# Value weights multiplied into the output weights, and attention over the latent rows: one edit to a hybrid encoder-layer kernel

## The chip, the cores and the metric

The program runs on one core of one Trainium2 chip. What is compared is the device time of one execution in microseconds (us), the median of several runs. TensorE (PE in the profile) does the matmuls, VectorE (DVE), ScalarE (ACT) and GpSimd (POOL) the elementwise work; SyncE (SP) issues nearly all DMA transfers, ACT's queue a few. Each engine executes its own instructions strictly in order and waits for the others on semaphores.

## The reference, cut to what matters

One encoder layer over 2048 tokens of width 1024, in float32. Two head groups work on one input projection `z`: a bidirectional mLSTM and a latent attention (MLA) with 4 heads. Their outputs are joined, multiplied by `w_out` and added to `x`; a feed-forward block follows. The part that the change touches:

```python
kv = (rms_norm(c_kv, g_ckv) @ w_ukv).reshape(B, S, A_HEADS, A_NOPE + A_DV)   # 128 -> 4 x (128 + 128)
k_nope, v = kv[..., :A_NOPE], kv[..., A_NOPE:]
...
s = jnp.einsum('bhqd,bhkd->bhqk', q_blk, kh) * scale
p = jax.nn.softmax(s, axis=-1)
out = jnp.einsum('bhqk,bhkv->bhqv', p, vh)
...
x = x + jnp.concatenate([y_a, y_b], axis=-1) @ w_out[l]                      # y_b = out, 4 x 128 columns
```

The latent `c_kv` has 128 columns, and it is the same for all heads; a head's value is `c_kv @ Wv_h` with a 128x128 matrix. Since `p @ (c Wv_h) @ Wo_h = (p @ c) @ (Wv_h Wo_h)`, the value projection of the tokens can be replaced by a product of two weight matrices for each head.

## The kernel before, in words

Every float32 matrix product is done as three matmuls on operands split into a high part (rounded to the matmul's format, a cast on ACT) and a low part (the rest, a subtraction on DVE or POOL): `split` (L53, L54; with a gain L56, L57) makes the parts, `mm3` (L69 to L71) issues the matmuls high x high, high x low, low x high. Tiles have 128 partitions and up to 512 columns.

The program has four stages, with places that matter here in the first two.

1. **Input stage** (`phase_a`, to about 458 us of the profile). Two halves of 8 token tiles (128 tokens each). A half first projects each tile onto the "rest" columns (gates, latents, rotary key), then runs three blocks of 8 steps with the weights of the mLSTM's values (`z_v`), queries and keys (`z_qk`) and output gate (`z_o`). A step is 24 matmuls into a bank `pz`. `tick` hangs the MLA work of a tile between the steps: `mla_a1` normalises the latents (`cn`) and transposes them, `mla_a2` multiplies them by `w_ukv` (two banks of 512 columns, tiles `wukh`, `wukl`, result `pm`) and `w_uq`, `mla_b1` and `mla_b2` apply norms and rotary factors and store queries and keys; `mla_b1` also copies the values out (L369) and stores them to `d_va` (L371). The last `z_qk` blocks end with a convolution, `ot`, that is transposed (L464), copied (`kt`, one buffer, L466 and L478) and stored to `d_k` (L471, L472, L479). The order on each engine in this stage is chosen by the framework's scheduler from its own cost estimates, so an edit can move instructions anywhere in the stage, up to the first rows of the next one.
2. **Attention** (`attention`, about 458 to 1110 us). The order is the written one. Step g of 256 computes one 128x512 block of scores, five matmuls into one of three banks `ps` (L1090 to L1094); DVE scales it, takes the maximum and frees the bank (L1095); ACT applies the exponential (L1106). From step 16 on, blocks of probabilities are transposed (`ptp`, L1137) and split, from step 22 on multiplied with the values (`pv`). Keys are loaded and split once a head, and so are values (`load_v`, `split_v`: 4 tiles for each of 4 heads). `work` is a generator that issues one piece of the mLSTM for each step: its first 28 pieces (`mlstm_prelude`) work out the gate tables in short chains on PE, DVE and ACT, with steps in which nothing is issued; the rest (`mlstm_steps`) are the chunks. The prelude's matmuls use the two banks `pm`.
3. **Output projection** (`OutProj`): `concat(y_a, y_b) @ w_out`, with Strassen-like products. It loads the rows of `w_out` below 512 for `y_b` at L1381 and L1497.
4. **Feed-forward** (`FeedForward`), untouched.

SP's queue is in order: a DMA instruction that waits for its data or its buffer holds up all that are behind it.

Of the kernel before, what the change touches and what calls it, by code (L numbers as in the profile page):

```python
# [88 lines left out]
def scratch(c, ctx):  # L89
# [9 lines left out]
    c.d_kr = dr.tile([NH, ROPE, S], F32, name="d_kr")  # L99
    c.d_va = dr.tile([S, 512], F32, name="d_va")  # L100
    c.d_ya = dr.tile([S, 512], F32, name="d_ya")
# [17 lines left out]
def phase_a(c):  # L119
    nc, tc = c.nc, c.tc  # L120
    with ExitStack() as st:
# [136 lines left out]
        def load_wu():  # L258
            for k in range(2):
                for j in range(2):  # L260
                    raw = rp.tile([P, 512], F32, name="raw")
                    cs = slice(j * 384, (j + 1) * 384)
                    nc.sync.dma_start(raw[:, :384], c.w_uq[k * P:(k + 1) * P, cs])
                    split(nc, wuqh[k][:, cs], wuql[k][:, cs], raw[:, :384], gcq[:, k:k + 1])
            for j in range(2):
                raw = rp.tile([P, 512], F32, name="raw")
                cs = slice(j * 512, (j + 1) * 512)
                nc.sync.dma_start(raw, c.w_ukv[:, cs])
                split(nc, wukh[:, cs], wukl[:, cs], raw, gcq[:, 2:3])

# [38 lines left out]
        def mla_a1(t, zr):  # L309
# [18 lines left out]
            with urgent():  # L328
                split(nc, ch, cl, pt[:, 0:3, :])
            mla_env[t] = [zr, ms3, ch, cl]  # L330

        def mla_a2(t):

            zr, ms3, ch, cl = mla_env[t]
            pk, pq = [], []
            for j in range(2):
                o = psM.tile([P, 512], F32, name="pm")
                cs = slice(j * 512, (j + 1) * 512)
# [11 lines left out]
            qs = [pq[h // 2][:, (h % 2) * DH:(h % 2 + 1) * DH] for h in range(NH)]  # L350
            ks = [pk[h // 2][:, (h % 2) * 256:(h % 2) * 256 + NOPE] for h in range(NH)]
            for h in range(NH):
# [7 lines left out]
            rsqrt(c, r8, ms8, 8)  # L360
            mla_env[t] = [zr, pk, qs, ks, r8]

        def mla_b1(t):

            tok = slice(t * P, (t + 1) * P)
            zr, pk, qs, ks, r8 = mla_env[t]
            vn = mp.tile([P, NH, DV], F32, name="vn")
            for j in range(2):
                nc.scalar.copy(vn[:, 2 * j:2 * j + 2, :],  # L369
                               pk[j].rearrange("p (h d) -> p h d", h=2)[:, :, NOPE:])  # L370
            nc.sync.dma_start(c.d_va[tok, :], vn.rearrange("p h d -> p (h d)"))  # L371
            kpe = mp.tile([P, 1, ROPE], F32, name="kpe")
# [141 lines left out]
        rbs = {}  # L514
# [18 lines left out]
        for half in range(2):  # L533
# [35 lines left out]
            for blk in range(3):  # L569
# [35 lines left out]
def mlstm_prelude(c, psM):  # L605
# [4 lines left out]
    with ExitStack() as st:  # L610
# [111 lines left out]
        stores(1)  # L722
        yield


# [13 lines left out]
def mlstm_steps(c, pool, ps, ld):  # L739
# [185 lines left out]
    for n, grp in enumerate(groups):  # L925
        outs = [outer(kws.pop(ch), ld.pop(ch)[0]) for ch in grp]
        yield
        for k, ch in enumerate(grp):
            new = back[ch - 1] = advance(1, NT - 1 - ch, outs[k])
            if ch > 4:  # L930
                nc.sync.dma_start(c.d_C[ch - 1], new)
                ld[ch - 4] = mlstm_v(c, ch - 4), mlstm_k(c, ch - 4)
            if k == 0 and n + 1 < len(groups):
# [69 lines left out]
def attention(c, keep, drain, project):  # L1003

    nc, tc = c.nc, c.tc
    with ExitStack() as st:
# [41 lines left out]

        def load_v(h, j):
            raw = vraw[h, j] = rp.tile([P, 512], F32, name="raw").rearrange("p (k d) -> p k d", k=4)  # L1050
            nc.sync.dma_start(raw, c.d_va[j * 512:(j + 1) * 512, h * DV:(h + 1) * DV].rearrange(
                "(k p) d -> p k d", p=P))

        def split_v(h, j):
            raw = vraw.pop((h, j))
# [3 lines left out]
            V[h, j] = vh, vl  # L1059

# [80 lines left out]
        def pv(b, j, k):  # L1141
            h = b // NB
# [3 lines left out]
            vh, vl = V[h, j]  # L1146
            if b < N - 1:
# [34 lines left out]
        load_v(0, 0)  # L1182
        load_v(0, 1)
        work = mlstm()
        def next_v(bp, j):
            h = bp // NB + 1
            if bp % NB == NB - 1 and h < NH:
                split_v(h, j)
                if j < 2:
                    load_v(h, j + 2)  # L1190

        for g0 in range(0, 16 * N, 2):
# [4 lines left out]
            for g in pair:  # L1197
                bp, n = divmod(g - 22, 16)
                if bp >= 0:
                    pv(bp, *divmod(n, 4))  # L1200
                    if n % 4 == 3:
                        next_v(bp, n // 4)
            if g0 % 16 == 4 and g0 > 32:
                out(g0 // 16 - 2)()
            for g in pair:
# [8 lines left out]
                if h < NH - 1 and i == 7 and u in (4, 5, 6):  # L1214
                    split_k(h + 1, u - 3, nc.vector if u == 6 else nc.gpsimd)
                    if u == 6:
                        load_v(h + 1, 0)
                        load_v(h + 1, 1)
                if g >= 16:
# [13 lines left out]
                if h < NH - 1:  # L1233
# [4 lines left out]
                    if i == 6 and u in (4, 5, 6):  # L1238
                        load_k(h + 1, u - 3)
                if g in (6, 8, 10, 12):  # L1240
                    split_v(0, g // 2 - 3)
                    if g < 10:
                        load_v(0, g // 2 - 1)
            if g0 == 16 * N - 10:
# [96 lines left out]
class OutProj:  # L1341
# [19 lines left out]
    def weights(self):  # L1361
# [132 lines left out]
    def load_b2(self, half):  # L1494
        for k in range(4):
            self.c.nc.sync.dma_start(self.c.e[:, 4 * (1 - half) + k, :],
                                     self.c.w_out[(4 + k) * P:(5 + k) * P, half * 512:(half + 1) * 512])  # L1497

# [848 lines left out]
```

## Time and profile before

| what | us |
|---|---|
| median of 3 runs | 2544.44 (2542.18 to 2544.75) |
| the profiled execution's own time | 2542.08 |
| its span, first to last instruction | 2540.3 |
| PE busy | 2523.7 (99%) |
| DVE busy | 1726.1 (68%) |
| ACT busy | 1293.7 (51%) |
| POOL busy | 380.7 (15%) |

The profile's busy time of an engine is the time covered by its instructions, whether or not they overlap; a matmul's row has its length from first to last column, and the next one may start before it ends. In lists of instructions by time the first column is the start, the second the length, and behind the instruction stands the idle time before it with what ended it; `x2` means that neighbours of one kind were merged into a row. `SPq` and `ACTq` are DMA instructions on those queues. The granted clock of TensorE is 1.00 in all windows.

### The profile page before, as it was taken

Reading aid. Unit: us, or ns where it says so; the run is one execution under the profiler, and the core shown is the slowest. Engines: PE = TensorE matmul, PEld = TensorE weight load, DVE = VectorE, ACT = ScalarE, POOL = GpSimd, SP = SyncE. Lnnn points to the kernel's source line nnn. Section 1 sums busy time; section 2 is a strip of 40 time slices with the busy share of each in tenths; the row PEclk is TensorE's granted clock in tenths of the full one; section 3 lists DMA queues with packets and bytes.
Section 4 is the critical chain, followed back from the end, with each engine's and each line's share of the span. In section 5 each row is a group of like instructions: output and inputs, shape, how many; then the busy total and the mean of one; then the engine's idle time right before and its main releaser. Section 6 shows DMA issues by size and latency. Waiting matters only on the chain. (4 is left out here: it accounts for less than half of the span.)

```text
span 2540.3 us, 35812 instructions
## 1 busy us (share of the span) xinstructions
PE 2523.7 (99%) x12380; PEld 2111.3 (83%) x12380; DVE 1726.1 (68%) x3286; ACT 1293.7 (51%) x2900; POOL 380.7 (15%) x428
## 2 busy tenths in 40 slices
PE   9999999999999999999999999999999999999999
PEld 7888888788888888888888888888888888888887
DVE  5585467766667667678788777977775577665433
ACT  6454444656767677674455555655554323332332
POOL 1211111223323332200000000000000232322000
PEclk9999999999999999999999999999999999999999
DMA  5434234355344343235786555654448544444552
GB/s 177 143 112 152 91 113 137 111 146 134 89 115 114 85 121 102 63 110 193 235 271 227 196 189 185 244 166 149 142 153 300 201 149 142 145 145 145 211 183 95
DMA packets 295931, 392.53 MB, mean 155 GB/s; under 512 B 32262, under 2 KB 176965, under 8 KB 295749
## 3 DMA queue, kind: packets, MB, share of 16 engines
q1 hardware_dynamic: 293284, 385.78, 48.0%
q10 hardware_dynamic: 2464, 4.46, 0.5%
q8 instruction: 97, 1.59, 0.3%
q14 instruction: 86, 0.70, 0.1%
HBM read 258.51 MB, written 131.64 MB: 154 GB/s over the span
## 5 line engine op out<-in xcount | busy, mean ns | idle before, releaser
L69 PE MATMUL pd<-w2h,uh 128*128 128x512 f32 x896 | 348.8, 389 | 0.1
L70 PE MATMUL pd<-w2l,uh 128*128 128x512 f32 x896 | 348.7, 389 | 0.0
L71 PE MATMUL pd<-w2h,ul 128*128 128x512 f32 x896 | 348.7, 389 | 0.0
L54 DVE TENSOR_TENSOR ul<-ur,uh 128x1024 fp32r<-128x1024 f32 x110 | 149.3, 1357 | 251.8 <-ACT uh L53 251.8
L53 ACT CAST uh<-ur 128x1024 fp32r<-128x1024 f32 x110 | 115.7, 1052 | 396.0 <-PE pd L70 382.4
L54 DVE TENSOR_TENSOR ptl<-ptp,pth 128x512 fp32r<-128x512 f32 x248 | 171.1, 691 | 190.0 <-ACT pth L53 188.9
L53 ACT CAST pth<-ptp 128x512 fp32r<-128x512 f32 x248 | 143.4, 578 | 157.7 <-PE ptp L1137 157.1
L2015 DVE TENSOR_TENSOR e<-pu,e 128x512 f32<-128x512 f32 x224 | 151.3, 689 | 88.7 <-PE pu L71 87.7
L69 PEld LDWEIGHTS pd<-w2h,uh 128*128 128x128 f32 x896 | 168.2, 188 | 35.4 <-DVE e L2015 0.5
L71 PEld LDWEIGHTS pd<-w2h,ul 128*128 128x128 f32 x896 | 168.2, 188 | 34.9
L70 PEld LDWEIGHTS pd<-w2l,uh 128*128 128x128 f32 x896 | 168.2, 188 | 34.8
L1106 ACT ACTIVATE p<-p,nm 128x512 f32<-128x512 f32 x256 | 185.8, 726 | 2.6 <-DVE nm L1099 2.6
L1095 DVE TENSOR_SCALAR_CACHE_REDUCE p<-ps 128x512 f32<-128x512 f32 x256 | 167.4, 682 | 15.2 <-PE ps L1094 15.1
L2179 POOL TENSOR_TENSOR r<-wr,r 128x512 f32<-128x512 f32 x48 | 81.5, 1697 | 621.1 <-DMA wr<-in_w 590.0
L69 PE MATMUL pz<-wh,hh 128*128 128x512 f32 (+1 forms) x384 | 149.5, 391 | 1.7 <-ACT vo L495 0.7
L71 PE MATMUL pz<-wh,hl 128*128 128x512 f32 (+1 forms) x384 | 150.0, 391 | 0.0
L70 PE MATMUL pz<-wl,hh 128*128 128x512 f32 (+1 forms) x384 | 149.2, 389 | 0.1
L2018 ACT ACTIVATE e<-e 128x512 f32<-128x512 f32 x128 | 80.9, 632 | 120.5 <-DVE e L2015 114.0
L1137 PE MATMUL ptp<-ident,p 128*128 128x128 f32 x992 | 130.6, 274 | 0.5 <-DVE ptl L54 0.3
L1137 PEld LDWEIGHTS ptp<-ident,p 128*128 128x128 f32 x992 | 113.6, 140 | 14.1 <-issue 1.4
L1090 PE MATMUL ps<-kh,qh 128*128 128x512 f32 x256 | 112.8, 441 | 2.4 <-DVE p L1095 2.4
L1883 ACT CAST r<-w1raw 128x512 fp32r<-128x512 f32 x104 | 64.6, 622 | 92.5 <-PE pu L71 92.5
(526 smaller groups left out, 6463.5 us busy)
## 6 DMA issues: line engine op xcount, KB each, us to landing
d_u<-e SPq DMA_DIRECT2D x224, 256.0 KB
ur<-d_u SPq DMA_DIRECT2D x110, 512.0 KB
wr<-in_w SPq DMA_DIRECT2D x96, 256.0 KB
w1raw<-in_w SPq DMA_DIRECT2D x42, 512.0 KB
raw<-in_w_in SPq DMA_DIRECT2D x48, 256.0 KB
r<-in_w SPq DMA_DIRECT2D x22, 512.0 KB
mb<-d_M SPq DMA_DIRECT2D x32, 256.0 KB
acc<-d_x SPq DMA_DIRECT2D x16, 512.0 KB
```

Source lines behind the costliest of these rows:

```text
L53: r = nc.scalar.copy(hi, src)
L54: (eng or nc.vector).tensor_tensor(lo, src, hi.bitcast(F32), op=ALU.subtract)
L69: nc.tensor.matmul(out, ah, bh, start=first, stop=False, skip_group_check=more)
L70: nc.tensor.matmul(out, ah, bl, start=False, stop=False, skip_group_check=more)
L71: nc.tensor.matmul(out, al, bh, start=False, stop=last, skip_group_check=more)
L1090: nc.tensor.matmul(o, qh[:, qs], kh, start=True, stop=False)
L1095: nc.vector.tensor_scalar(p, o, SCALE, None, op0=ALU.mult, op1=ALU.max, accum_out=maxes[b, a][:, j:j + 1])
L1106: nc.scalar.activation(p, p, AF.Exp, bias=maxes[b, a], accum_out=dens[b][:, a, j:j + 1])
L1137: nc.tensor.transpose(pt[:, k, :], p[:, k * P:(k + 1) * P], c.ident)
L2015: nc.vector.tensor_tensor(out, o, t, op=ALU.add)
L2018: nc.scalar.activation(t, t, AF.Relu)
L2179: nc.gpsimd.tensor_tensor(R, wr, R, op=ALU.subtract)
```

## The change

* `mla_a2` multiplies the latents by the key columns of `w_ukv` alone: `wukh` and `wukl` hold 512 columns (head by head the first 128 of 256), one bank instead of two. The normalised latent `cn[:, 256:384]` is stored to a new array `d_cn` (64 KB a tile) from ACT's queue. `mla_b1` no longer copies values out, and `d_va` is gone.
* `value_rows`, new, works out `Wv_h Wo_h` for the 4 heads: it loads the value columns of `w_ukv` (`wv`), multiplies them by the norm's gain on POOL, transposes them on PE (4 transposes), splits them, and for each of 8 pieces (head, half of the columns) loads 128x512 of `w_out` (`wraw`), splits it (ACT, POOL: `wo0`, `wo1`), issues three matmuls into `pm`, copies the result out on DVE and stores it to `d_wv`. It is a generator beside the prelude: both advance once a step. Its transposes come at step 3 (counted from 0), the first split of a piece at step 4, products 0 to 4 at steps 6, 8, 10, 12, 14 and products 5 to 7 at steps 22, 24, 26. Like the prelude it has 28 pieces.
* Attention uses `d_cn` as the values of all heads: `load_v` and `split_v` run 4 times instead of 16, at steps 2 to 8 and 16 to 22.
* The first mLSTM loads (`d_v`, `d_k`) are issued at step 10 instead of step 0, later ones one piece earlier.
* One more of the three key splits at a head's end runs on DVE instead of POOL.
* The output projection reads its lower rows from `d_wv`.
* In the input stage, `x` tiles have 3 buffers instead of 2; tiles 8 to 10 are loaded at step 3 of the third block of the first half, and tiles 11 to 15 three tiles ahead.

```diff
-        xp = pool("a_x", 2, "right")
+        xp = pool("a_x", 3, "right")
...
         def mla_a2(t):
-            zr, ms3, ch, cl = mla_env[t]
-            pk, pq = [], []
-            for j in range(2):
-                o = psM.tile([P, 512], F32, name="pm")
-                cs = slice(j * 512, (j + 1) * 512)
-                mm3(nc, o, ch[:, 2, :], cl[:, 2, :], wukh[:, cs], wukl[:, cs], True, True)
-                pk.append(o)
+            zr, ms3, ch, cl, cn = mla_env[t]
+            nc.scalar.dma_start(c.d_cn[t * P:(t + 1) * P, :], cn[:, 256:384])
+            pq = []
+            pk = psM.tile([P, 512], F32, name="pm")
+            mm3(nc, pk, ch[:, 2, :], cl[:, 2, :], wukh[:, 0:512], wukl[:, 0:512], True, True)
...
         def mla_b1(t):
-            vn = mp.tile([P, NH, DV], F32, name="vn")
-            for j in range(2):
-                nc.scalar.copy(vn[:, 2 * j:2 * j + 2, :],
-                               pk[j].rearrange("p (h d) -> p h d", h=2)[:, :, NOPE:])
-            nc.sync.dma_start(c.d_va[tok, :], vn.rearrange("p h d -> p (h d)"))
...
+            elif 8 <= t < 13:
+                xts[t + 3] = load_x(t + 3)
...
+                    if half == 0 and blk == 2 and i == 3:
+                        for t in range(8, 11):
+                            xts[t] = load_x(t)
...
+def value_rows(c, pool, psM):
+    outs = [tile([P, 512], F32, name=f"wst{i}") for i in range(2)]
+    pieces = [tile([P, 512], F32, name=f"wraw{i}") for i in range(3)]
+    raw = tile([P, NH, P], F32, name="wv")
+    wvh, wvl = (tile([P, NH, P], F32R, name=f"wv{u}") for u in "hl")
+    homes = [[tile([P, 512], F32R, name=f"wo{i}{u}") for u in "hl"] for i in range(2)]
...
+    def load(n):
+        if n < 2 * NH:
+            r, cs = place(n)
+            nc.sync.dma_start(pieces[n % 3], c.w_out[512:][r, cs])
+
+    def part(n):
+        if n < 2 * NH:
+            split(nc, *homes[n % 2], pieces[n % 3], eng=nc.gpsimd)
+            load(n + 3)
+
+    nc.sync.dma_start(raw, c.w_ukv.rearrange("p (h t d) -> p h t d", h=NH, t=2)[:, :, 1, :])
+    for n in range(3):
+        load(n)
+    for _ in range(2):
+        yield
+    nc.gpsimd.tensor_scalar(raw, raw, c.vec[:, 10:11], None, op0=ALU.mult)
+    yield
+    pt = psM.tile([P, 512], F32, name="pm").rearrange("p (k t) -> p k t", k=4)
+    for h in range(NH):
+        nc.tensor.transpose(pt[:, h, :], raw[:, h, :], c.ident)
+    yield
+    split(nc, wvh, wvl, pt)
+    part(0)
+    yield
+    yield
+    store = None
+    for n in range(2 * NH):
+        o = psM.tile([P, 512], F32, name="pm")
+        mm3(nc, o, wvh[:, n // 2, :], wvl[:, n // 2, :], *homes[n % 2], True, True)
+        if store:
+            nc.sync.dma_start(*store)
+        yield
+        w = outs[n % 2]
+        nc.vector.tensor_copy(w, o)
+        store = c.d_wv[place(n)], w
+        part(n + 1)
+        yield
+        for _ in range(6 if n == 4 else 0):
+            yield
+    nc.sync.dma_start(*store)
...
-            ld = {ch: (mlstm_v(c, ch), mlstm_k(c, ch)) for ch in range(NT - 1, NT - 5, -1)}
-            yield from mlstm_prelude(c, psM)
+            with ExitStack() as s_fold:
+                fold = value_rows(c, pool("w_sb", 1, "left", s_fold.enter_context), psM)
+                for n, _ in enumerate(mlstm_prelude(c, psM)):
+                    next(fold, None)
+                    if n == 10:
+                        ld = {ch: (mlstm_v(c, ch), mlstm_k(c, ch)) for ch in range(NT - 1, NT - 5, -1)}
+                    yield
+                for _ in fold:
+                    yield
...
-                    split_k(h + 1, u - 3, nc.vector if u == 6 else nc.gpsimd)
+                    split_k(h + 1, u - 3, nc.gpsimd if u == 4 else nc.vector)
...
-            nc.sync.dma_start(raw, c.w_out[k * P:(k + 1) * P, :])
+            nc.sync.dma_start(raw, c.d_wv[(k - 4) * P:(k - 3) * P, :])
```

Three places where the order of instructions moves. The first is PE in the middle of the input stage, where one token tile's latents (`cTh`, `cTl`) meet the key and value weights (`wukh`, `wukl`) and the query weights (`wuqh`, `wuql`). Before:

```order
L69 MATMUL pm<-wukh,cTh 128x512
L70 MATMUL pm<-wukl,cTh 128x512
L69 MATMUL pm<-wukh,cTh 128x512
L70 MATMUL pm<-wukl,cTh 128x512
L69 MATMUL pm<-wuqh_152,cTh 128x384
L70 MATMUL pm<-wuql_154,cTh 128x384
```

Now, at the last tile:

```order
L69 MATMUL pm<-wukh,cTh 128x512
L70 MATMUL pm<-wukl,cTh 128x512
L69 MATMUL pm<-wuqh_153,cTh 128x384
L71 MATMUL pm<-wukh,cTl 128x512
L70 MATMUL pm<-wuql_155,cTh 128x384
```

A tile issues three matmuls with `wukh` and `wukl` instead of six (before, the two with `cTl` follow some rows later).

The second is SP's queue where the input stage ends: `ot` and `kt` are the last convolution blocks of the mLSTM's keys, `v` and `knat` the mLSTM's first loads, `wv` and `wraw` the new loads. Before:

```order
L459 DMA d_qkT<-ot 128x514
L479 DMA d_k<-kt 2x128
L471 DMA d_k<-kt 128x128
L472 DMA d_k<-kt 128x3x128
L728 DMA v_4979<-d_v 128x4x128
L479 DMA d_k<-kt 2x128
L735 DMA knat_4983<-d_k 128x256
```

Now:

```order
L453 DMA d_qkT<-ot 128x514
L465 DMA d_k<-kt 128x128
L466 DMA d_k<-kt 128x3x128
L473 DMA d_k<-kt 2x128
L750 DMA wv<-in_w_ukv 128x4x128
L743 DMA wraw_4973<-in_w_out 128x512
```

The load of `wv` stands directly behind the last store of `kt`, where the first load of `d_v` and `d_k` stood around it.

The third is PE at the start of attention: `pz` is the last step of the input stage, `ps` a block of scores, `pt<-ident,ot` the transposes from which `kt` is copied, `pm<-ident,G` the prelude's first matmuls. Before:

```order
L69 MATMUL pz<-wh,hh 128x512
L464 MATMUL pt<-ident,ot 128x128 x4
L476 MATMUL pt<-ident,ot 2x128
L70 MATMUL pz<-wl,hh 128x512
L71 MATMUL pz<-wh,hl 128x512
L69 MATMUL pz<-wh,hh 128x512
L70 MATMUL pz<-wl,hh 128x512
L71 MATMUL pz<-wh,hl 128x512
L1094 MATMUL ps<-rl,qr 128x512
```

Now, from the second block of scores on:

```order
L1151 MATMUL ps<-rl,qr 128x512
L458 MATMUL pt<-ident,ot 128x128 x4
L470 MATMUL pt<-ident,ot 2x128
L627 MATMUL pm<-ident,G 64x128
L628 MATMUL pm<-rev,G 64x128
L627 MATMUL pm<-ident,G 64x128
L628 MATMUL pm<-rev,G 64x128
L1147 MATMUL ps<-kh,qh 128x512
```

The last transposes of `ot` moved from before the first block of scores to behind the second; two blocks of scores later the four transposes of `wv` follow:

```order
L1149 MATMUL ps<-kh,ql 128x512
L1150 MATMUL ps<-rh,qr 128x512
L1151 MATMUL ps<-rl,qr 128x512
L759 MATMUL pm<-ident,wv 128x128 x4
L1147 MATMUL ps<-kh,qh 128x512
```

So PE has those four transposes between the fourth and the fifth block of scores.

More of the change, by code (lines that the diff above doesn't have):

```diff
@@ L99, in scratch @@
     c.d_kr = dr.tile([NH, ROPE, S], F32, name="d_kr")
-    c.d_va = dr.tile([S, 512], F32, name="d_va")
+    c.d_cn = dr.tile([S, P], F32, name="d_cn")
+    c.d_wv = dr.tile([NH * P, D], F32, name="d_wv")
     c.d_ya = dr.tile([S, 512], F32, name="d_ya")
@@ L266, in load_wu @@
                 raw = rp.tile([P, 512], F32, name="raw")
-                cs = slice(j * 512, (j + 1) * 512)
-                nc.sync.dma_start(raw, c.w_ukv[:, cs])
-                split(nc, wukh[:, cs], wukl[:, cs], raw, gcq[:, 2:3])
+                nc.sync.dma_start(raw, c.w_ukv[:, j * 512:(j + 1) * 512])
+                cs = slice(j * 256, (j + 1) * 256)
+                split(nc, *[w[:, cs].rearrange("p (h d) -> p h d", h=2) for w in (wukh, wukl)],
+                      raw.rearrange("p (h t d) -> p h t d", h=2, t=2)[:, :, 0, :], gcq[:, 2:3])
         def z_nat(hts, tl, w, n):
@@ L329, in mla_a1 @@
                 split(nc, ch, cl, pt[:, 0:3, :])
-            mla_env[t] = [zr, ms3, ch, cl]
+            mla_env[t] = [zr, ms3, ch, cl, cn]
         def mla_a2(t):
-            zr, ms3, ch, cl = mla_env[t]
-            pk, pq = [], []
-            for j in range(2):
-                o = psM.tile([P, 512], F32, name="pm")
-                cs = slice(j * 512, (j + 1) * 512)
-                mm3(nc, o, ch[:, 2, :], cl[:, 2, :], wukh[:, cs], wukl[:, cs], True, True)
-                pk.append(o)
+            zr, ms3, ch, cl, cn = mla_env[t]
[3 more added lines that the diff above has]
+            mm3(nc, pk, ch[:, 2, :], cl[:, 2, :], wukh[:, 0:512], wukl[:, 0:512], True, True)
             for j in range(2):
@@ L350, in mla_a2 @@
             qs = [pq[h // 2][:, (h % 2) * DH:(h % 2 + 1) * DH] for h in range(NH)]
-            ks = [pk[h // 2][:, (h % 2) * 256:(h % 2) * 256 + NOPE] for h in range(NH)]
+            ks = [pk[:, h * NOPE:(h + 1) * NOPE] for h in range(NH)]
             for h in range(NH):
@@ L360, in mla_a2 @@
             rsqrt(c, r8, ms8, 8)
-            mla_env[t] = [zr, pk, qs, ks, r8]
+            mla_env[t] = [zr, qs, ks, r8]
         def mla_b1(t):
-            tok = slice(t * P, (t + 1) * P)
-            zr, pk, qs, ks, r8 = mla_env[t]
-            vn = mp.tile([P, NH, DV], F32, name="vn")
-            for j in range(2):
-                nc.scalar.copy(vn[:, 2 * j:2 * j + 2, :],
-                               pk[j].rearrange("p (h d) -> p h d", h=2)[:, :, NOPE:])
-            nc.sync.dma_start(c.d_va[tok, :], vn.rearrange("p h d -> p (h d)"))
+            zr, qs, ks, r8 = mla_env[t]
             kpe = mp.tile([P, 1, ROPE], F32, name="kpe")
@@ L723, in mlstm_prelude, with place @@
         yield
+def value_rows(c, pool, psM):
+    nc = c.nc
+    tile = pool.tile
+    outs = [tile([P, 512], F32, name=f"wst{i}") for i in range(2)]
[3 more added lines that the diff above has]
+    homes = [[tile([P, 512], F32R, name=f"wo{i}{u}") for u in "hl"] for i in range(2)]
+    def place(n):
+        h, j = divmod(n, 2)
+        return slice(h * P, (h + 1) * P), slice(j * 512, (j + 1) * 512)
+    def load(n):
[36 more added lines that the diff above has]
+    nc.sync.dma_start(*store)
 def mlstm_v(c, ch):
@@ L926, in mlstm_steps @@
         outs = [outer(kws.pop(ch), ld.pop(ch)[0]) for ch in grp]
+        for ch in grp:
+            if ch > 4:
+                ld[ch - 4] = mlstm_v(c, ch - 4), mlstm_k(c, ch - 4)
         yield
@@ L1047, in split_k, with load_v, split_v @@
             K[h, j] = kh, kl, rh, rl
[L1049 to L1055, printed above, removed]
+        def load_v(j):
+            raw = vraw[j] = rp.tile([P, 512], F32, name="raw").rearrange("p (k d) -> p k d", k=4)
+            nc.sync.dma_start(raw, c.d_cn[j * 512:(j + 1) * 512, :].rearrange("(k p) d -> p k d", p=P))
+        def split_v(j):
+            raw = vraw.pop(j)
             vh = vp.tile([P, 4, DV], F32R, name="vh")
@@ L1058, in split_v @@
             split(nc, vh, vl, raw, eng=nc.gpsimd)
-            V[h, j] = vh, vl
+            V[j] = vh, vl
         def load_q(h, j):
@@ L1141, in pv @@
         def pv(b, j, k):
-            h = b // NB
             if (j, k) == (0, 0):
@@ L1145, in pv @@
             th, tl = pts[b, j]
-            vh, vl = V[h, j]
+            vh, vl = V[j]
             if b < N - 1:
@@ L1181, in attention @@
             split_k(0, j, nc.gpsimd if j == 2 else nc.vector)
-        load_v(0, 0)
-        load_v(0, 1)
         work = mlstm()
[L1185 to L1190, printed above, removed]
         for g0 in range(0, 16 * N, 2):
@@ L1239, in attention @@
                         load_k(h + 1, u - 3)
[L1240 to L1243, printed above, removed]
+                if g in (2, 4, 6, 8):
+                    load_v(g // 2 - 1)
+                if g in (16, 18, 20, 22):
+                    split_v(g // 2 - 8)
             if g0 == 16 * N - 10:
@@ L1496, in load_b2 @@
             self.c.nc.sync.dma_start(self.c.e[:, 4 * (1 - half) + k, :],
-                                     self.c.w_out[(4 + k) * P:(5 + k) * P, half * 512:(half + 1) * 512])
+                                     self.c.d_wv[k * P:(k + 1) * P, half * 512:(half + 1) * 512])
     def cast(self, n, name):
```

6 lines of the change are left out of this document (removed).

## The prediction

> **What bounds the kernel now.** I read the page's busy line first, then what PE (TensorE) waited for, then windows of the two places that the change touches, then the times of single matmuls there.
>
> ```profile
> PE 2523.7 (99%) x12380; PEld 2111.3 (83%) x12380; DVE 1726.1 (68%) x3286; ACT 1293.7 (51%) x2900; POOL 380.7 (15%) x428
> PE pt L204 <- DMA rows<-in_g_mix: 4.5, 1, 4.5
> PE ps L1090 <- DVE p L1095: 2.4, 4, 1.3
> PE pt L325 <- DVE cn L321: 1.4, 1, 1.4
> PE pz L69 <- ACT vo L495: 0.7, 1, 0.7
> ```
>
> PE is busy for 2523.7 of 2540.3 us, and the rows of its waits (total, times, longest) are short: 4.5 us at the very start, 2.4 us at blocks of scores, 0.7 us at the bank `pz`. PE is the bound nearly everywhere, so an edit counts by what PE issues, and by new waits on PE. The windows (PE, PEld, DVE, ACT, POOL busy) say where that is not so:
>
> ```profile
> 100.00:200.00 100.00, 100.00 (x493) 85.02 (x492) 77.90 (x206) 51.54 (x166) 17.44 (x25) 1.00 0.42 131
> 470.00:475.00 5.00, 4.31 (x21) 3.12 (x19) 4.58 (x17) 3.10 (x9) 2.12 (x2) 1.00 1.04 261
> 475.00:480.00 5.00, 3.88 (x17) 2.58 (x15) 4.96 (x13) 4.27 (x11) 4.37 (x4) 1.00 0.37 92
> ```
>
> In the input stage PE is covered without a gap, while DVE is at 78%. In the opening of attention there is a stretch of 10 us where DVE is busy 4.58 and 4.96 of 5 us and PE idles 0.69 + 1.12 us: there DVE is the bound, and the new work lands near it.
>
> Third, the price of a matmul. A row's length is not what it costs:
>
> ```profile
> 162.15 0.40 PE L69 MATMUL pm<-wukh,cTh 128*128 128x512 f32 x1
> 162.39 0.40 PE L70 MATMUL pm<-wukl,cTh 128*128 128x512 f32 x1
> 162.62 0.39 PE L69 MATMUL pm<-wukh,cTh 128*128 128x512 f32 x1
> 162.85 0.39 PE L70 MATMUL pm<-wukl,cTh 128*128 128x512 f32 x1
> L69 PE MATMUL pm<-wukh,cTh x32: 390/396/505, 57.5 to 416.7; 128*128 128x512 f32 x32
> ```
>
> These are the very matmuls that the change thins out. Each row lasts 0.40 us, but the next starts 0.23 us behind it ((162.85 - 162.15) / 3). The rows of attention further down give the same: from 461.31 to 463.60 stand two blocks of five matmuls, 2.29 / 10 = 0.229 us. That is my price; the 0.396 of the row's length is kept as a rival.
>
> **The change, part by part.**
>
> *Removed in the input stage.* The last row has x32: two for each of 16 tiles, and so have those with `wukl` and `cTl`. Half of the 96 go: 48 x 0.229 = **-11.0 us**. PE has no gap there, so all of it should come off, unless something else is late (a rival below).
>
> *Added to PE.* Eight products of three matmuls: 24 x 0.229 = **+5.5 us**. The four transposes of `wv` I price by the five of `ot` below, 0.47 us from 456.26 to 456.73, less one: **+0.4 us**.
>
> *A new wait.* PE's transposes of `wv` stand behind the fourth block of scores, and `wv` is loaded behind the last store of `kt` on SP's in-order queue. How long each chain takes can be read from the last `ot` in the trace before, with P0 = 456.26, the start of its transposes:
>
> ```profile
> 456.26 0.60 PE L464 MATMUL pt<-ident,ot 128*128 128x128 f32 x4
> 456.73 0.47 PE L70 MATMUL pz<-wl,hh 128*128 128x512 f32 x1
> 459.44 0.32 PE L628 MATMUL pm<-ident,G 128*64 128x128 f32 x1
> 460.03 0.50 PE L1090 MATMUL ps<-kh,qh 128*128 128x512 f32 x1
> 461.31 0.39 PE L1090 MATMUL ps<-kh,qh 128*128 128x512 f32 x1
> 463.60 0.39 PE L1090 MATMUL ps<-kh,qh 128*128 128x512 f32 x1
> 456.94 0.59 ACT L466 COPY kt<-pt 128x512 f32<-128x512 f32 x1 [2.99 <-PE pt L464]
> 457.95 0.44 SPq L472 DMA_DIRECT2D d_k<-kt  x1
> 460.18 0.26 ACT L478 COPY kt<-pt 2x128 f32<-2x128 f32 x1 [1.42 <-DMA d_k<-kt]
> 460.46 0.24 SPq L479 DMA_DIRECT2D d_k<-kt  x1
> ```
>
> PE's side: after the change the order is `ot` transposes (0.47), the matmuls with `G` (460.03 - 459.44 = 0.59), two blocks of scores (463.60 - 461.31 = 2.29), then `wv`. PE is there at P0 + 3.35. The load's side: `kt` is copied, stored, its one buffer waited for (1.42 us on the store), filled again and stored, and SP is free at 460.46 + 0.24 = 460.70, P0 + 4.44. Only then is `wv` issued. PE is past the point before the load has even begun. How long the load and the gain's product take, by the nearest rows:
>
> ```profile
> 52.44 0.33 SPq L268 DMA_DIRECT2D raw<-in_w_ukv  x1
> 55.54 0.72 ACT L56 ACTIVATE wukh<-raw,vec 128x512 fp32r<-128x512 f32 x1 [1.65 <-DMA raw<-in_w_ukv]
> 467.82 1.09 SPq L1051 DMA_DIRECT2D raw<-d_va  x2
> 473.55 0.62 ACT L53 CAST vh<-raw 128x512 fp32r<-128x512 f32 x1 [1.90 <-DMA raw<-d_va]
> L54 POOL TENSOR_TENSOR vl<-raw,vh x16: 1267/1280/1367, 468.4 to 1005.1; 128x512 fp32r<-128x512 f32 x16
> L756 POOL TENSOR_TENSOR kw<-knat,gn x30: 615/622/657, 504.1 to 1026.3; 128x256 f32<-128x256 f32 x30
> ```
>
> A load of 256 KB of the same array took 55.54 - 52.44 = 3.1 us from issue to its waiting user; a load in the same stretch of attention, with others around it, 473.55 - 467.82 = 5.7; the store of `kt` above 460.18 - 457.95 = 2.2. I take 3.1, the same array and size: P0 + 7.5. POOL's product of 128x512 by a gain: a two-operand row of that size is 1.28, the 128x256 one doubled 1.24; I take 1.3: P0 + 8.8. PE's wait is 8.8 - 3.35 = **+5.5 us**, between 4.6 (load of 2.2) and 8.1 (load of 5.7); 3.9 if the two blocks of scores hold PE up by 0.7, as `vo` once did. Behind the waiting transposes stand the fifth block of scores and all that follows on PE; DVE and ACT run dry, so nothing hides it. The Trainium skill (DMA: Bandwidth & Descriptors, "Anatomy of one DMA — SWDGE (gpsimd) path") gives about 2.0 us fixed and the bytes over the bandwidth, my estimate 2.6 us for these 256 KB, with which the sum would be 0.5 lower. That page's fit is for another issuing path than SP's, and the row of 3.1 has the whole of this one; it stays in the sum.
>
> *DVE in the opening.* DVE gets five result copies of 128x512 and one subtraction before step 16, 6 x 0.69 by the `p` row below = 4.1 us; PE gets five products there and the transposes, 5 x 0.69 + 0.4 = 3.8. Where DVE is the bound (windows above), its 4.1 takes the place of PE's 3.8, and the idle 1.8 us stays. I take 0, from -0.7 (the wait pushes the scores away from the long DVE scans) to +1.5 (a copy lands ahead of a score's `p`).
>
> ```profile
> 476.20 3.45 DVE L671 TENSOR_TENSOR_SCAN mr<-g 1x15 f32<-1x15 f32 x8
> 485.28 0.69 DVE L1095 TENSOR_SCALAR_CACHE_REDUCE p<-ps 128x512 f32<-128x512 f32 x1
> L369 ACT COPY vn<-pm x32: 351/365/401, 62.7 to 420.6; 128x256 f32<-128x256 f32 x32
> 459.73 0.33 ACTq L497 DMA_DIRECT2D d_sg<-vo  x1
> ```
>
> *Edits at nothing.* The 32 copies `vn` (11.7 us of ACT, at 52% in the first window) and their stores go, and 16 issues of `d_cn` come onto ACT's queue at 0.33 us: both lie under PE's matmuls; without that cover the issues cost 5.3 us. Twelve value loads and splits fewer, on SP, ACT and POOL: PE never waited on them. Three key splits moved from POOL to DVE, two pieces each: 3 x 2 x 0.69 = 4.1 us under PE over 650 us. The mLSTM loads of step 10 have 18 steps until their use. `d_wv` has the size of `w_out`'s rows. `x` in a third buffer: no row of PE's waits names `x`.
>
> *Sum.* -11.0 + 5.5 + 0.4 + 5.5 = **+0.4 us**. The profiled execution took 2542.08, so 2542.5; the median shown stands 2.36 above it: **2544.9 us**.
>
> **The rivals.**
>
> *No wait at `wv`* (the load lands in time, or PE comes late enough for other reasons). Then the count of matmuls decides: -5.1, 2539.3. Against it: SP's free time is after PE's arrival by any row. For it: the scheduler that placed `ot` may have the input stage end otherwise than the rows before.
>
> *The input stage's tail is late.*
>
> ```profile
> 433.43 0.38 PE L413 MATMUL pt<-ident,kr 128*128 128x128 f32 x2
> 453.37 0.75 DVE L455 SCALAR_TENSOR_TENSOR ot<-acc,cb,sg 128x514 f32<-128x514 f32 x1 [0.86 <-ACT sg L452]
> ```
>
> The last `ot` is done 454.12 - 433.43 = 20.7 us behind the last key transposes, a chain of DVE and ACT. After the change PE reaches the `ot` transposes after 74 matmuls of `pz` (16.9), two earlier sets of transposes (0.9) and two blocks of scores (2.3), 20.1 us: too early by 0.6, by 2 if DVE is held up by a score's `p`. That price comes on top of the wait for `wv` (it moves both sides): 2546.5.
>
> *Slower: ACT held by its new DMAs.* ACT is in order; a `d_cn` issue in front of a `vo` copy (it frees `pz`) costs PE its 0.33 once ACT lags by more than a step, 24 x 0.229 = 5.5 us. If each of the 16 strikes: 5.3 + 0.4, so 2550.2. For it: PE did wait for `vo` once. Against: ACT's queue has 16 `d_sg` issues of the same kind today with that one wait of 0.7, and ACT loses 11.7 us of copies.
>
> *Matmuls cost their rows' length*: 24 fewer at 0.396 is -9.5 in place of -5.5: 2540.9 with the wait, 2535.3 without it, the lowest of all cases. The starts 0.23 us apart speak against it. So does the Trainium skill (Perfetto Trace Analysis, "Identifying the Most-Contended Engine"), which calls the matmuls' busy share a poor measure because they are pipelined; by it the forecast's -5.5 stands.
>
> **How the numbers follow.** The forecast 0.52, no wait 0.16, the tail 0.14, ACT held 0.12, row lengths 0.06. What a measurement of this kernel can tell from no change is about 0.2%, 5.1 us: 2539.3 to 2549.5. Faster: about half of the no-wait case, which ends on that bound, and of the row lengths (0.11), and a little for gains that I cost at nothing: 0.14. Slower: ACT held, and the tail with a load of 5.7 us: 0.15. The same: 0.71. The likeliest case by itself spans 2543 (load 2.2, DVE -0.7) to 2549 (5.7, +1.5). The range takes in the no-wait case with some room, and ACT held: 2538.0 to 2550.5.
>
> **What would show it.** Matmul rows `pm<-wukh,cTh` x16 and an input stage shorter by about 11 us; 24 rows `pm<-wvh` some 0.23 us apart; in PE's waits a new row of some 5.5 us for `pm<-ident,wv`, ended by POOL's product; ahead of it `wv` issued some 4.4 us behind the last `ot` transposes' start. The forecast is wrong if that row is under 3.9 or over 8.1 us, if PE shows waits for `cn` or `vo` in the input stage, or if the two idle stretches of the opening grow by more than 1.5 us.

## The result, and the profile after

| kernel | median, us (runs) | against the kernel before, 95% interval |
|---|---|---|
| before | 2544.60 (6) | |
| changed | 2554.97 (6) | 1.0043 (1.0030 to 1.0056) |

The change makes the kernel 10.4 us slower. The forecast was 2544.9 us, no change, within 2538.0 to 2550.5; the result lies above that range. The profiled execution of the changed kernel took 2554.66 us, with a span of 2552.9; TensorE's mean granted clock was 0.998, where it was 1.00 before.

PE's waits (total, times, longest) in the changed kernel, those that are new or longer:

```profile
PE pm L759 <- POOL wv L755: 6.4, 1, 6.4
PE pm L716 <- DVE rv L714: 2.6, 1, 2.6
PE ps L1147 <- DVE p L1152: 2.1, 2, 1.7
PE pt L458 <- DVE ot L449: 1.0, 1, 1.0
PE pz L69 <- ACT vo L489: 0.8, 2, 0.7
```

The first row is the wait that was forecast. The second and much of the third were not. To see where time is lost, I follow the start of the same block of scores (its first matmul; blocks are counted from 0) through the traces. The column "no fold" is the changed kernel without the fold, from an experiment below.

| block of scores | before | changed | no fold | changed minus no fold |
|---|---|---|---|---|
| 3 | 461.31 | 452.55 | 453.60 | -1.0 |
| 4 | 462.46 | 460.99 | 454.75 | +6.2 |
| 6 | 464.73 | 465.31 | 457.02 | +8.3 |
| 18 | 482.68 | 483.80 | 474.58 | +9.2 |
| 24 | 494.13 | 500.03 | 487.03 | +13.0 |
| 28 | 504.28 | 516.07 | 497.18 | +18.9 |
| 255 | 1110.33 | 1122.43 | 1103.48 | +18.9 |

The input stage's gain is there: at block 3 the changed kernel is 8.8 us ahead of the kernel before. By block 28, within 64 us, the gain is gone and the changed kernel is 11.8 us behind; little moves after that (12.1 us at block 255, 12.6 at the end of the span). Against the kernel without the fold the loss falls into three places: 7 us at the wait (blocks 3 to 4) and 2 right behind it, 4 between blocks 18 and 24, 6 between blocks 24 and 28.

**Blocks 3 to 6.** Windows of the changed kernel (PE, PEld, DVE, ACT, POOL busy; then the granted clock):

```profile
454.00:456.00 2.00, 0.00 (x0) 0.00 (x0) 0.90 (x4) 1.54 (x2) 0.00 (x0) 1.00 0.00 1
456.00:458.00 2.00, 0.00 (x0) 0.00 (x0) 0.00 (x0) 0.31 (x1) 0.00 (x0) 1.00 0.66 212
458.00:460.00 2.00, 0.00 (x0) 0.00 (x0) 0.00 (x0) 0.00 (x0) 1.42 (x1) 0.59 0.80 258
460.00:462.00 2.00, 1.78 (x7) 1.59 (x8) 0.00 (x0) 0.63 (x2) 0.17 (x1) 0.50 0.95 274
462.00:464.00 2.00, 2.00 (x6) 1.61 (x5) 0.49 (x1) 1.97 (x3) 1.28 (x1) 0.50 0.64 170
...
466.00:468.00 2.00, 2.00 (x10) 1.67 (x9) 1.97 (x6) 1.23 (x4) 0.69 (x1) 1.00 0.86 261
```

PE is empty from 454 us on, and towards the end of the gap its granted clock falls to 0.50, where it stays until about 465 us. The matmuls behind the gap show it in the timeline:

```profile
449.99 0.66 PE L458 MATMUL pt<-ident,ot 128*128 128x128 f32 x4 [1.01 <-DVE ot L449]
...
460.22 1.11 PE L759 MATMUL pm<-ident,wv 128*128 128x128 f32 x4 [6.35 <-POOL wv L755]
460.99 0.78 PE L1147 MATMUL ps<-kh,qh 128*128 128x512 f32 x1
461.56 0.63 PE L1148 MATMUL ps<-kl,qh 128*128 128x512 f32 x1
461.99 0.63 PE L1149 MATMUL ps<-kh,ql 128*128 128x512 f32 x1
...
465.31 0.39 PE L1147 MATMUL ps<-kh,qh 128*128 128x512 f32 x1
```

Starts lie 0.43 us apart in place of 0.23. The ten matmuls of blocks 4 and 5 take 465.31 - 460.99 = 4.32 us instead of 2.29: 2.0 us lost. I had not costed that at all. The Trainium skill has the rule (TensorE: Matmul & The Clock Gate, "Part 1: The HAM clock gate (the "warmup" mystery)"): after an idle window of about 3.4 us, whose position does not follow the kernel, the array runs at half its clock until a busy window has passed. This trace agrees: 4.5 us of idle time before the fall (453.87 to 458.35), then 6.8 us of half clock. It spoke against this change, and the prediction did not weigh it.

**Blocks 18 to 24.** DVE and SP around 480 us:

```profile
474.72 0.57 SPq L784 DMA_DIRECT2D v<-d_v  x1
...
479.09 0.62 SPq L791 DMA_DIRECT2D knat<-d_k  x1
479.80 0.38 SPq L743 DMA_DIRECT2D wraw<-in_w_out  x1
480.28 0.38 SPq L770 DMA_DIRECT2D d_wv<-wst  x1
485.58 0.69 DVE L773 COPY wst<-pm 128x512 f32<-128x512 f32 x1 [3.67 <-DMA d_wv<-wst]
486.93 0.50 PE L1147 MATMUL ps<-kh,qh 128*128 128x512 f32 x1 [1.70 <-DVE p L1152]
```

The results of the products are copied into two tiles in turn, and each is stored from there. The store of product 2 was issued at 480.28 us, behind eight loads of the mLSTM. The copy of product 4 needs that tile, and DVE stands still for 3.67 us until the store has landed. The next block's `p` is late by it, and so PE.

**Blocks 24 to 28.** PE and DVE of the changed kernel, and then the same place before:

```profile
503.88 0.65 PE L711 MATMUL pm<-rev,x 128*64 128x128 f32 x4
504.46 0.50 PE L69 MATMUL pm<-wo0h,wvh 128*128 128x512 f32 x1
...
505.26 1.03 PE L1194 MATMUL ptp<-ident,p 128*128 128x128 f32 x8
508.92 0.56 PE L716 MATMUL pm<-x,rev 128*128 128x192 f32 x2 [2.62 <-DVE rv L714]
508.37 0.41 DVE L714 COPY rv<-pm 64x256 f32<-64x256 f32 x1
```

```profile
497.97 0.65 PE L712 MATMUL pm<-rev,x 128*64 128x128 f32 x4
498.55 1.09 PE L1137 MATMUL ptp<-ident,p 128*128 128x128 f32 x8
499.48 0.49 PE L717 MATMUL pm<-x,rev 128*128 128x192 f32 x2
501.71 0.41 DVE L715 COPY rv<-pm 64x256 f32<-64x256 f32 x1
```

Before, the prelude's last two matmuls used the two banks `pm` in turn: the second ran at 499.48, while DVE read the first's bank only at 501.71. Now a product stands between them and takes the second bank. So the last matmul needs the first bank, which is free only when DVE has copied `rv`, and that copy stands behind two subtractions `ptl` which wait for ACT. PE waits 2.62 us, and once more the clock falls (3.4 us at half clock cost 1.7; products 6 and 7, which lie here too, are another 1.4 of the 6 us):

```profile
506.00:509.00 3.00, 0.38 (x4) 0.17 (x3) 1.71 (x3) 2.96 (x7) 1.28 (x2) 1.00 1.29 46
509.00:511.00 2.00, 2.00 (x7) 1.67 (x8) 0.19 (x1) 0.00 (x0) 0.65 (x1) 0.64 0.35 55
511.00:513.00 2.00, 2.00 (x7) 1.52 (x6) 1.19 (x3) 0.00 (x0) 0.00 (x0) 0.51 0.18 12
```

One thing must be known to compare totals. At the head of all these executions the starts of matmuls lie farther apart than later (in the kernel before 0.39 to 0.55 us until 8.4 us, 0.21 from 8.7 us on), and how long that lasts differs: summed over the starts in the first 20 us, waits included, against the median distance for their shape, the excess is 2.5 us in the profile of the kernel before, 3.8 in that of the changed kernel, and between 2.8 and 5.6 in those of the experiments. So single profiles are compared from place to place, and totals by medians.

### The profile page after: what moved, and what is told of

The parts are those of the page before. It is cut to its first block, busy times and chain, and to the rows that moved or that the text cites. A ratio compares the mean times of both kernels' runs of the same rounds, so it can differ in the third digit from the quotient of the medians.

```text
span 2552.9 us, 35713 instructions
## 1 busy us (share of the span) xinstructions
PE 2524.8 (99%) x12360; PEld 2111.3 (83%) x12360; DVE 1735.0 (68%) x3301; ACT 1287.1 (50%) x2865; POOL 372.4 (15%) x419
```

## The experiments

All are edits of the changed kernel (2554.97), each with a median of 5 to 11 runs.

### The fold left out

```diff
-                fold = value_rows(c, pool("w_sb", 1, "left", s_fold.enter_context), psM)
+            fold = iter(())
...
-            nc.sync.dma_start(raw, c.d_wv[(k - 4) * P:(k - 3) * P, :])
+            nc.sync.dma_start(raw, c.w_out[k * P:(k + 1) * P, :])
```

The output projection's other load of these rows, half of the columns at a time, is changed in the same way.

> The changed kernel without the fold: no loads, transposes, products and stores of it, and the output projection reads the unfolded weights, so that part of the computation is left out. It shows what the input stage and the shared values alone gain. By my count of matmuls 11.0 us less than the kernel before, of which the trace of the changed kernel has shown 1.1 lost at the start and 1.0 at the last convolution block: 2544.6 - 8.9 = 2535.7. If loads and splits of the values that fell away help attention too, below 2535; if the shortened input stage is late elsewhere, above 2538.

Measured: 2536.80, 0.9970 (0.9959 to 0.9982). The input stage and the shared values gain 7.8 us by medians; the fold costs 18.2 where I had forecast 11.4. The waits of this kernel name one loss:

```profile
PE ps L1147 <- DVE p L1152: 2.2, 3, 1.6
PE pt L458 <- DVE ot L449: 1.9, 1, 1.9
```

PE now reaches the last convolution block 1.9 us before it is done (1.0 in the changed kernel's profile, 0.2 to 2.1 in those of the experiments that keep the order), the rival that I had priced at 0.6 to 2. With 1.9 us of it the count gives -9.1, within the interval (-10.4 to -4.6). The other 1.3 us, or more in executions where that wait is shorter, are not resolved; the edits that I had put at nothing are in this run too.

### The value columns loaded early

```diff
-    raw = tile([P, NH, P], F32, name="wv")
+    raw = stage.tile([P, 512], F32, name="raw").rearrange("p (h t) -> p h t", h=NH)
...
+        s_fold = ExitStack()
+        fold = value_rows(c, pool("w_sb", 1, "left", s_fold.enter_context), psM, rp)
+        next(fold)
         work = mlstm()
```

(The first `next` issues the loads of `wv` and of the first three pieces, behind the first key loads.)

> The changed kernel, with the loads of the value columns and of the first three pieces of the output weights issued right behind the first key loads, into tiles of the staging pool, instead of behind the last store of the keys. Nothing else is moved on TensorE. Theory A (the wait for the value columns costs its own 6.4 us and about 2.4 us more, because the granted clock is 0.50 for some 6 us behind it): no wait at the four transposes, clock 1.00 from 446 to 480 us, about 8.7 us less than the changed kernel, 2546.3. Theory B (the clock falls for another reason, the start of attention): 6.4 us less, 2548.6, and the clock still falls. Theory C (VectorE sets the opening's pace, the wait only lets it catch up): VectorE's waits come back in place of it, 2 us less or nothing, 2553 to 2555.

Measured: 2548.24, 1.0014 (1.0005 to 1.0022), 6.7 us less. No wait at the transposes is left, and in the window around them the clock is 1.00:

```profile
456.00:466.00 10.00, 8.41 (x38) 6.27 (x36) 7.42 (x23) 8.65 (x18) 1.27 (x1) 1.00 0.43 137
```

Among PE's waits, new ones at the products stand in its place:

```profile
PE pm L70 <- POOL wo1l L54: 0.9, 1, 0.9
PE pm L70 <- POOL wo0l L54: 0.8, 1, 0.8
PE pm L69 <- ACT wo0h L53: 0.7, 1, 0.7
```

At block 6 the trace is 6.7 us ahead of the changed kernel's, though it came 1.4 us later to block 0: 8.1 us, near theory A's 8.7. Some 4 of it are lost again between blocks 6 and 10, 2.4 of them in the three waits above: the products now come before ACT and POOL have split their operands. Another 2.2 us of lead come between blocks 18 and 20: the copy of product 4, which stood still for 3.67 us in the changed kernel, waits here for PE only (1.05 us). So neither A nor C alone: the wait and its half clock go, a part returns as other waits, and the 6.7 us hold some of the tile's price too. That the total is near theory B's 2548.6 is chance, since the clock at the transposes does not fall. It does fall later, behind the wait for `rv`, as in the changed kernel.

### TensorE kept busy through the wait

```diff
+    for _ in range(26):
+        nc.tensor.matmul(flat, wa, wb, start=True, stop=True)
     for h in range(NH):
         nc.tensor.transpose(pt[:, h, :], raw[:, h, :], c.ident)
```

> The changed kernel with 26 matmuls of 512 columns, whose result nobody reads, ahead of the four transposes of the value columns, so that TensorE works through most of the wait (26 x 0.227 = 5.9 us of its 6.4). Theory A (idle time brings the clock down): the clock stays at 1.00, the wait shrinks to about 0.5 us, and the time is about 2.4 us below the changed kernel, 2552.6. Theory B (the clock falls for another reason): the clock still falls and the time is that of the changed kernel, 2555.0.

Measured: 2554.35, 1.0040 (1.0027 to 1.0052): within the scatter of the changed kernel. The trace says why. The clock did fall, but earlier, behind the wait for `ot`; its row in the timeline, and the windows behind it:

```profile
452.18 0.66 PE L458 MATMUL pt<-ident,ot 128*128 128x128 f32 x4 [1.77 <-DVE ot L449]
```

```profile
454.00:456.00 2.00, 2.00 (x6) 1.52 (x6) 0.67 (x3) 1.79 (x3) 0.00 (x0) 0.50 0.68 206
456.00:458.00 2.00, 2.00 (x8) 1.58 (x7) 0.74 (x3) 1.41 (x3) 0.00 (x0) 0.68 0.01 3
458.00:460.00 2.00, 2.00 (x11) 1.65 (x10) 0.64 (x4) 0.56 (x2) 0.00 (x0) 1.00 0.54 159
```

Behind the filled wait the clock is 1.00, as theory A says, but this time the wait of 1.77 us for `ot` brought it down. That left B possible, so the next run fills that gap too.

```diff
+            if (b, a, j) == (0, 0, 1):
+                for _ in range(9):
+                    nc.tensor.matmul(o, qh[:, qs], kh, start=True, stop=True)
```

> The kernel of the run before with 26 idle-filling matmuls ahead of the value columns' transposes, and 9 more inside the second block of scores, so that TensorE meets the last convolution block's transposes about 2 us later and does not wait there either. Theory A (idle time brings the clock down): the clock stays at 1.00 from 440 to 500 us; the fillers cost nothing to 1 us beyond the two waits that they fill, and the half clock's 2.4 us are saved: 2552.6 to 2553.6. Theory B (attention's opening itself brings it down): the clock falls once more between 446 and 466 us, and the time is 2555 or more.

Measured: 2555.88, 1.0043 (1.0031 to 1.0056). The clock is 1.00 through the whole of attention's start, from before the `ot` transposes to behind those of `wv`:

```profile
452.00:456.00 4.00, 4.00 (x26) 3.08 (x25) 2.17 (x8) 2.19 (x4) 0.00 (x0) 1.00 0.54 183
456.00:460.00 4.00, 4.00 (x20) 3.29 (x19) 1.06 (x6) 2.15 (x4) 0.00 (x0) 1.00 0.33 102
460.00:464.00 4.00, 2.66 (x14) 1.93 (x12) 0.00 (x0) 0.00 (x0) 1.58 (x1) 1.00 0.71 234
```

So B falls: attention's start does not lower the clock, idle time on PE does (a rest of 1.3 us of wait did not). The total does not show the saving. Its profile came 1.8 us later to block 0 and fell to half clock at 490.9 us, behind a wait of 2.0 us for DVE; 1.2 us above the changed kernel at block 6 is what 1.8 at the start, 1.0 of fillers beyond the `ot` wait and 0.8 beyond that for `wv` (26 x 0.227 + 1.3 - 6.35), less 2.4, come to. That the half clock costs time is thus read from the starts of matmuls, and not from a total.

### The wait alone

```diff
-    split(nc, wvh, wvl, pt)
-    part(0)
-    yield
-    yield
+    nc.vector.tensor_copy(wvh, pt)
+    return
...
```

The products and their stores are left out, and the output projection reads `w_out` as in the kernel without the fold.

> The changed kernel with the loads, the gain product and the four transposes of the value columns and nothing behind them: no products, and the output projection reads the unfolded weights, so that part of the computation is left out. It measures the wait alone against the kernel without any fold (2536.8). Theory A: 0.4 for the transposes, 6.4 of wait and 2.4 of half clock, 2546.0, of the 18.2 us between the two kernels 9.2. Theory B: 2543.6. If the wait only lets other engines catch up on work that TensorE would have waited for later: below 2542.

Measured: 2542.70, 0.9992 (0.9983 to 1.0001): 5.9 us above the kernel without a fold: below what theories A and B gave, 2546.0 and 2543.6, and just above 2542, below which it was to lie if the wait only lets other engines catch up. In its profile the wait is 6.1 us and the half clock begins earlier in it, at 457 us, so that less of it falls on work:

```profile
457.00:460.00 3.00, 0.00 (x0) 0.00 (x0) 0.00 (x0) 2.97 (x7) 0.74 (x1) 0.52 0.77 223
460.00:464.00 4.00, 3.10 (x10) 2.62 (x11) 0.00 (x0) 1.49 (x5) 0.84 (x1) 0.50 0.80 218
464.00:466.00 2.00, 2.00 (x10) 1.64 (x9) 1.37 (x5) 0.00 (x0) 0.00 (x0) 1.00 1.03 295
```

Against the kernel without a fold it is 8.1 us behind at block 6 and 6.2 at block 10: the PE wait of 1.6 us for a block's `p`, which stands in that kernel's rows above, does not occur, since DVE had caught up. Wait, transposes and half clock, less what DVE regained, come to 5.9 us. That this is the 5.5 + 0.4 of the forecast is luck: two parts that it did not have nearly cancel.

### Two steps more between products 5 and 6

```diff
-        for _ in range(6 if n == 4 else 0):
+        for _ in range(6 if n == 4 else 2 if n == 5 else 0):
```

> The changed kernel with products 6 and 7 two steps later (steps 26 and 28), so that no product takes a bank between the prelude's two matmuls with the reversal matrix. Theory D (the 2.6 us wait at the last of them is a matter of the two banks' turn, and the second fall of the clock follows from it): the wait for rv is gone, the clock is 1.00 around 510 us, some 4.3 us less, 2550.7. Rival (VectorE is late by then whatever the banks): the wait is found at the next matmul that needs VectorE, no change, 2555.

Measured: 2549.97, 1.0023 (1.0013 to 1.0033), 5.0 us less than the changed kernel. The row for `rv` is gone from PE's waits (that for `wv` remains, 6.0 us), and the clock holds where it fell before:

```profile
506.00:510.00 4.00, 4.00 (x20) 3.32 (x20) 3.11 (x9) 2.23 (x6) 1.21 (x1) 1.00 0.05 5
510.00:514.00 4.00, 4.00 (x23) 3.40 (x22) 2.06 (x5) 2.74 (x6) 0.31 (x1) 1.00 0.10 28
```

So it was the banks' turn, not DVE's pace.

### Four result tiles, or the mLSTM's loads later

```diff
-    outs = [tile([P, 512], F32, name=f"wst{i}") for i in range(2)]
+    outs = [tile([P, 512], F32, name=f"wst{i}") for i in range(4)]
...
-        w = outs[n % 2]
+        w = outs[n % 4]
```

> The changed kernel with four tiles instead of two for the products' results. Theory E (VectorE's stop of 3.7 us at a result copy, whose tile is still being stored because the store was issued behind eight loads of the mLSTM, costs TensorE its waits around 486 to 493 us): the stop is gone and the time is some 2.4 us less, 2552.5. Rival (VectorE had that time to spare): 2555.

```diff
-                    if n == 10:
+                    if n == 16:
                         ld = {ch: (mlstm_v(c, ch), mlstm_k(c, ch)) for ch in range(NT - 1, NT - 5, -1)}
```

> The changed kernel with the mLSTM's first eight loads issued at step 16 instead of step 10; TensorE's order is the same, and SP has the stores of products 2 and 3 ahead of the eight loads. Theory E (the store of product 2 was late because it stood behind these loads, 5.0 us on SP): VectorE's stop of 3.7 us at the copy of product 4 goes or falls below 1 us, and the time is 2.4 to 3.2 us less than the changed kernel, 2552, as with four result tiles. Rival (the store itself takes long, 5.3 us from issue to release in the trace, whatever stands before it): a stop of 2 us or more remains, 2554 to 2555.

Measured: 2551.74, 1.0027 (1.0016 to 1.0038), and 2551.83, 1.0029 (1.0019 to 1.0039): 3.2 and 3.1 us less than the changed kernel. With four tiles DVE's waits have no row for `wst` left. With the loads later, SP issues the store of product 2 at 476.32, and DVE's copy of product 4 has no wait:

```profile
476.32 0.32 SPq L770 DMA_DIRECT2D d_wv<-wst  x1
481.80 0.69 DVE L773 COPY wst<-pm 128x512 f32<-128x512 f32 x1
```

So the stop was due to the eight loads ahead of the store. A stop of 3.3 us remains in this kernel at a later product.

### All three, and a version with more room

The kernel with early loads, four result tiles and the later products, and then besides:

```diff
-    part(0)
-    yield
-    yield
+    part(0)
+    yield
+    part(1)
+    yield
...
-        part(n + 1)
+        part(n + 2)
```

> Early loads, four result tiles and products 6 and 7 two steps later, all at once. If the three causes are separate and the list is complete, what is left beside the kernel without a fold is 24 matmuls and four transposes, 2536.8 + 5.9 = 2542.7. From the run with early loads alone, less the 4.3 to 5.0 us that the later products gave: 2543.2 to 2543.9. Above 2546: another wait comes up, at the products' operands on GpSimd (0.7 to 0.9 us each in the run with early loads).

> The kernel with early loads, four result tiles and the later products 6 and 7, and besides the pieces of the output weights split one product further ahead (piece n + 2 behind product n), so that GpSimd has two more steps for each. If the waits for GpSimd (0.9 us twice in the profile of the run before) and for the casts are all that is left of the fold beside its matmuls, 1.8 us less than that run, 2541.0, and faster than the kernel before by 0.15%. Rival (VectorE's pace in the opening shows up in place of them): 2542.8, no change.

> Once more the kernel with early loads, four result tiles, later products 6 and 7 and the splits further ahead, to tell whether it stands below the kernel before: 2542.0 to 2543.3, 0.05 to 0.1% faster, by what the kernel without a fold (2536.8) and 5.9 us of matmuls say 2542.7.

Measured: 2542.78, 0.9992 (0.9983 to 1.0001) for all three; 2543.33, 0.9996 (0.9987 to 1.0005), with the splits further ahead; 2544.21, 0.9999 (0.9991 to 1.0008), for the latter once more. PE's waits with all three:

```profile
PE pt L458 <- DVE ot L449: 1.7, 1, 1.7
PE pm L70 <- POOL wo0l L54: 0.9, 1, 0.9
PE pm L70 <- POOL wo1l L54: 0.9, 1, 0.9
```

2542.78 - 2536.80 = 6.0 us above the kernel without a fold: the 5.9 of 24 matmuls and four transposes. That nothing is seen beside them is partly chance: 1.8 us of waits for POOL (above) are new, and the 2.2 us that the kernel without a fold waits for `p` are gone. Taken out one at a time the three causes gave 6.7, 3.2 and 5.0 us, 14.9 in all; together they give 12.2, since the early loads alone had part of the tile's gain already. The further step did not lower the median. None of the three can be told from the kernel before; what the fold's own matmuls leave of the 7.8 us is 1 to 2 us.

### The token tiles as before

```diff
-        xp = pool("a_x", 3, "right")
+        xp = pool("a_x", 2, "right")
...
-            elif 8 <= t < 13:
-                xts[t + 3] = load_x(t + 3)
...
-                    if half == 0 and blk == 2 and i == 3:
-                        for t in range(8, 11):
-                            xts[t] = load_x(t)
```

> The changed kernel with the token tiles as before: two buffers, and no loads ahead in the first half's third block. My count says that this part is worth nothing: 2555.0. If the loads ahead kept the scheduler's order or the weights' loads from being late, up to 2 us more, 2557; if they delayed the weights, up to 2 us less, 2553.

Measured: 2554.17, 1.0034 (1.0021 to 1.0047), 0.8 us below the changed kernel and not to be told from it (the five runs reach from 2549.66 to 2555.33). The total shows no worth of the third buffer and the loads ahead, but they do move the order: without them the last transposes of `ot` stand ahead of the first block of scores again, as before the change, `wv` is issued at 451.54 instead of 455.06, and PE's wait for it is 2.3 us in this profile, which is that of the fastest of the five runs.

## Why the prediction was wrong

* **What bounds the kernel, and the price of a matmul: right.** The fold's matmuls, freed of waits, and four transposes cost 6.0 us by medians, where 5.5 + 0.4 was forecast at 0.229 for each matmul. By the rows' length it would have been 9.9, so that rival is out.
* **Removed, -11.0: mis-sized in effect.** 7.8 us by medians, 3.2 less than the term. The matmuls went (rows `pm<-wukh,cTh` from 32 to 16), and 0.2 to 2.1 us came back at the last `ot`, depending on the execution (1.9 in the profile without the fold); the rest is open. I had this as a rival with 0.14 and a price of 0.6 to 2, to be added to the forecast; it should have been a term of the sum, since its own working had PE early.
* **The new wait, +5.5: right.** 6.4 in the profile, 6.0 to 6.5 in the experiments that keep it and the order ahead of it (2.3 with the token tiles as before, where `wv` is issued earlier). PE came at P0 + 3.7 (forecast 3.35), `wv` was issued at 455.06, P0 + 5.1 (4.44), and the transposes began at 460.22, P0 + 10.2 (8.8). Two parts of the account were missing and nearly cancel, which is luck: the half clock behind the wait, some 2 us, and as much that DVE catches up.
* **DVE in the opening, 0, from -0.7 to +1.5: this is the step that failed.** I counted the instructions that DVE and PE get, and not what the products share with others. Two such things cost 8 us where I had allowed 1.5: the tile of a result that is still being stored, 3.1 to 3.2, and the bank `pm` that a product takes out of the prelude's turn, 5.0 with the half clock behind it. The second lies at products 6 and 7, behind the opening, where the sum had no term but the matmuls.
* **Edits at nothing: one was wrong.** Of the mLSTM's loads at step 10 I looked at when they are needed, and not at what stands behind them on SP: the store of product 2. That is the 3.1 us above. Of the others, `x` is tested and shows nothing in the total, though it moves the order where the input stage ends. The rest is not shown by a run of its own: PE's waits name no `vn` and no value split, but 1.3 us or more of the input stage's gain are unexplained.
* **The slower rival, ACT held by its DMAs: did not happen.** PE's wait for `vo` is 0.8 us, as before. The sign of the result was that of a case I had at 0.15, and its mechanism was none of mine.
* **The sum with what the runs showed:** -7.8 for the input stage and the shared values, +5.9 for the wait, +5.5 for the products, +3.1 for the tile, +5.0 for the bank: +11.7, against 10.4 measured. The parts overlap (14.9 us one at a time, 12.2 together), and medians scatter by about 1 us.

## What to carry to other kernels

Work that is put into another piece's unused tiles takes part in their turn: write down, for each ring of banks or tiles that the new work draws from, which tile it takes, who must have read it, and where that reader or its store stands in its own queue. A wait on the engine that bounds the kernel costs more than its length if the clock follows, so even 2 to 3 us of it are worth a table of who is late. And measure the part that gains apart from the part that pays: without the fold this change gains 7.8 us, and the best fold found pays 6 of it back.

## What was not expected of the hardware

The granted clock fell to 0.50 behind single waits of 6.4 and 2.6 us (changed kernel), 2.3 and 2.1 us (token tiles as before), 2.1 us (all three with the splits further ahead, once more), 2.0 us (second filled run) and 1.8 us (first filled run). It did not fall behind waits of 1.9 us (without the fold), 1.7 us (all three) and 2.6 us (for `rv`, in the second filled run and in those with the later loads and with the token tiles as before). The Trainium skill (TensorE: Matmul & The Clock Gate, "HAM oscillation — how this bites in real kernels") warns of gaps above about 3.4 us; here shorter ones were enough, in some executions.

The traces' records of the clock tell more than the windows above. Within every execution profiled here, a stretch at half clock lasted 3.41 or 6.83 us (leaving out the last, which the end of the program cuts off), and every fall and rise lay a whole number of 3.41 us behind the first record of full clock: in the changed kernel full clock begins at 11.21 us, and the falls at 458.35 and 509.55 lie 131 and 146 such steps behind it. If each profile is cut into these steps, each step at full clock in which PE was idle for 2.0 us or more ended with a fall. Those with up to 1.9 us did not, but for one with 1.73 us (first filled run). So one and the same wait of 2.62 us for `rv` lowered the clock where it lay within one step (changed kernel) and not where a step's end parted it into 1.42 and 1.20 us (later loads). The first record of full clock lay between 8.6 and 13.6 us in these profiles, so which of the two happens cannot be read from the program.
